# Gate and up strips of two FFNs: one matmul over 128 rows, or two row tiles of 64 rows side by side

## The chip, the cores and the metric

The kernel runs on one core of one Trainium2 chip. The metric is the device time in microseconds (us) of one execution, from the first to the last instruction; lower is better. The core has five engines that run their own instruction queues: TensorE (PE in the profile, with its weight loads listed apart as PEld), VectorE (DVE), ScalarE (ACT), GpSimd (POOL) and SyncE (SP, which here issues the DMAs). Matmuls read weights and moving data from SBUF and write sums to PSUM, of which this kernel uses eight banks: four tiles named acc and four named sm.

## The reference

One layer of a decoder step, in fp32, on 320 tokens (256 of a prompt, 64 of samples), model width 2048, FFN width 5632:

```python
x = x + 0.5 * swiglu_ffn(rmsnorm(x, n_f1), f1_g, f1_u, f1_d)     # (silu(h @ wg) * (h @ wu)) @ wd
m, s_new, buf_new = mixer(rmsnorm(x, n_mix), ...)                # HGRN2 heads + conv module
x = x + m
x = x + cross_attn(rmsnorm(x, n_xa), mk, mv, xa_q, xa_o)
x = x + 0.5 * swiglu_ffn(rmsnorm(x, n_f2), f2_g, f2_u, f2_d)
y = rmsnorm(x, final)
```

Only the products with the gate and up weights (2048 x 5632 each, in both FFNs) are touched by the change.

## The kernel before

Activations stand transposed: 16 tiles `xs[k]` of 128 features by T = 320 tokens. Weights stream from HBM in units of 128 x 1024 (tile `raw`, 512 KB, three buffers). ACT casts each unit to fp32r (`whi`, L116), DVE computes the rest that the cast lost (`wlo`, L117), and both go to TensorE; `whi` and `wlo` have four buffers each. Activations are split in the same way: `xgh`, `xgl` for the inputs of a projection, `hh`, `hl` for the FFN's inner values.

`mm3` (L176 to L178) multiplies one 128 x 128 block of weights with 320 tokens in three fp32r matmuls that add up in one PSUM bank: whi by xh, whi by xl, wlo by xh. `strip` makes one strip of 128 output features: 16 blocks, so 48 matmuls over two units.

`ffn` runs the FFN in six parts of 8, 8, 8, 8, 8 and 4 strips (`PARTS`). Within a part it makes a gate strip and an up strip for each of the eight; after the gate strip DVE multiplies the PSUM sum with `r`, the inverse root mean square (tile fa, L242), ACT takes Silu (L243), DVE multiplies by `r` again (L244); after the up strip DVE multiplies its PSUM sum with that (tile fb, L249) and `split` makes hh on ACT and hl on DVE. Then come the part's down products: 16 sums `ps` of 24 matmuls each (12 in the last part), which DVE adds to `xs[n]` (L259). One FFN thus has 88 strips, 4224 matmuls, and 2112 matmuls of down products.

The order on each engine is set by a scheduler at build time: instructions follow the program's order as far as their inputs are expected to be there; the units' fetches (DMA, L116, L117) have high priority and so stand early. Each engine then runs its queue strictly in that order. The rest of the program, about a quarter of the time between the FFNs, is the mixer and the cross attention; there are short fp32 matmuls among its strips (L512, L514, L584 and others), which run in two passes each. Some of them are already laid out on parts of the array: L584 takes 64 rows at a time, alternately the lower and the upper half of the partitions, into two PSUM tiles, and L556, L742 and L770 use 32 columns at a time.

Of the kernel before, what the change touches and what calls it, by code (L numbers as in the profile page):

```python
# [14 lines left out]
ALU = mybir.AluOpType  # L15
AX = mybir.AxisListType

P = 128
DM = 2048
KT = DM // P  # L20
# [4 lines left out]
T = NP + NS  # L25
# [37 lines left out]
def hymba(tc, A, O):  # L63
    nc = tc.nc
    count = [0]

    def tl(pool, shape, dt, tag, bufs):
        count[0] += 1
        return pool.tile(shape, dt, tag=tag, name=f"{tag}_{count[0]}", bufs=bufs)
# [9 lines left out]
    with (  # L79
# [8 lines left out]
        def acc():  # L88
            return tl(pp, [P, 512], F32, "acc", 4)

        def sm():
            return tl(pp, [P, 512], F32, "sm", 4)
# [6 lines left out]
        eps = cp.tile([P, 1], F32, name="eps")  # L99
# [15 lines left out]
        def split(hi, lo, src):  # L115
            nc.scalar.copy(hi, src)  # L116
            nc.vector.tensor_tensor(lo, src, hi.bitcast(F32), ALU.subtract)  # L117

        def pair(tag, w=T):
            return (tl(mp, [P, w], F32R, tag + "h", 16), tl(mp, [P, w], F32R, tag + "l", 17 if tag == "h" else 16))  # L120
# [5 lines left out]
        def fetch(early=False):  # L126
            with contextlib.nullcontext() if early else tc.high_priority():
                raw = tl(mp, [P, 1024], F32, "raw", 3)
                g, u = divmod(fetched[0], 2)
                nc.sync.dma_start(raw, A["w"][g, :, u * 1024 : (u + 1) * 1024])  # L130
                hi = tl(mp, [P, 1024], F32R, "whi", 4)
                lo = tl(mp, [P, 1024], F32R, "wlo", 4)
                split(hi, lo, raw)
                units.append((hi, lo))
            fetched[0] += 1

        def unit():
            while fetched[0] < 2 * G_TOT and fetched[0] < upos[0] + 4:
                fetch()
            u = units[upos[0]]  # L140
            units[upos[0]] = None
            upos[0] += 1
            return u
# [3 lines left out]
        def pump():  # L147
            for q in queues:
                q["due"] = q.get("due", 0) + q["rate"]
                while q["due"] >= 1:  # L150
                    q["due"] -= 1
                    while q["jobs"]:
                        try:
                            next(q["jobs"][0])
                            break
                        except StopIteration:
                            q["jobs"].pop(0)
# [9 lines left out]
        def tick(n):  # L167
            mms[0] += n
            if mms[0] >= pace[0]:
                mms[0] -= pace[0]  # L170
                pump()

        def mm3(out, w, kk, xh, xl, first, last):
            hi = w[0][:, kk * P : (kk + 1) * P]
            lo = w[1][:, kk * P : (kk + 1) * P]
            nc.tensor.matmul(out, hi, xh, start=first, stop=False)  # L176
            nc.tensor.matmul(out, hi, xl, start=False, stop=False)  # L177
            nc.tensor.matmul(out, lo, xh, start=False, stop=last)  # L178
            tick(1)

        def strip(xg, ps):
            for half in range(2):
                w = unit()
                for kk in range(8):
                    k = half * 8 + kk
                    mm3(ps, w, kk, *xg[k], k == 0, k == KT - 1)

        # r = (ps / n + eps) ** -0.5, the tables' value and one step of Newton's
        def root(r, ps, n):
            v = tl(mp, [P, r.shape[-1]], F32, "sq", 2)  # L190
            a = sm()[:, : r.shape[-1]]
# [40 lines left out]
        def ffn(pool, xg, root_of, done, setup=None):  # L232
            for pi, np_ in enumerate(PARTS):
                last_part = pi == len(PARTS) - 1
                hs = []
                for _ in range(np_):
                    pg = acc()
                    strip(xg, pg[:, :T])
                    if pi == 0 and not hs:
                        r = root_of()  # L240
                    t = tl(pool, [P, T], F32, "fa", 2)
                    nc.vector.tensor_tensor(t, pg[:, :T], r, ALU.mult)  # L242
                    nc.scalar.activation(t, t, AF.Silu)  # L243
                    nc.vector.tensor_tensor(t, t, r, ALU.mult)  # L244
                    pu = acc()
                    strip(xg, pu[:, :T])
                    hp = pair("h")
                    h = tl(pool, [P, T], F32, "fb", 2)
                    nc.vector.tensor_tensor(h, pu[:, :T], t, ALU.mult)  # L249
                    split(*hp, h)  # L250
                    hs.append(hp)
                w = None
                for n in range(KT):
                    if n * np_ % 8 == 0:
                        w = unit()
                    ps = acc()
                    for kk in range(np_):
                        mm3(ps[:, :T], w, n * np_ % 8 + kk, *hs[kk], kk == 0, kk == np_ - 1)
                    nc.vector.scalar_tensor_tensor(xs[n], ps[:, :T], 0.5, xs[n], ALU.mult, ALU.add)  # L259
                    if last_part:  # L260
                        done(n)
                if pi == 0 and setup is not None:
                    setup(pool)

        # first FFN
        nc.gpsimd.memset(ones, 1.0)
        nc.gpsimd.memset(eps, EPS)

# [6 lines left out]
        def setup(fp):  # L275
            nc.sync.dma_start(ident, A["ident"])
            nc.sync.dma_start(vmask, A["vmask"])
            nc.sync.dma_start(sel, A["sel"])
            for i0 in range(0, len(LEVELS), 3):
                i1 = min(i0 + 3, len(LEVELS))  # L280
                t = tl(fp, [P, 3, T], F32, "t4k", 2)
                nc.sync.dma_start(t[:, : i1 - i0], A["msk"][:, i0:i1, :])
                nc.vector.tensor_copy(msk[:, i0:i1, :], t[:, : i1 - i0])
            nc.gpsimd.memset(at[0], 0.0)
            nc.gpsimd.memset(at[1], 0.0)

            l0 = vec[:, V_LB : V_LB + NH]
            l1 = vec[:, V_LB + NH : V_LB + 2 * NH]
            lmax = cp.tile([P, NH], F32, name="lmax")
            le0 = cp.tile([P, NH], F32, name="le0")  # L290
            le1 = cp.tile([P, NH], F32, name="le1")
            nc.vector.tensor_tensor(lmax, l0, l1, ALU.max)
            nc.vector.tensor_tensor(le0, l0, lmax, ALU.subtract)
            nc.vector.tensor_tensor(le1, l1, lmax, ALU.subtract)
            nc.scalar.activation(le0, le0, AF.Exp)
            nc.scalar.activation(le1, le1, AF.Exp)
            nc.vector.tensor_tensor(le1, le0, le1, ALU.add)
            nc.vector.reciprocal(le1, le1)
            nc.vector.tensor_tensor(lb, le0, le1, ALU.mult)
            nc.vector.tensor_scalar(oml, lb, -1.0, 1.0, ALU.mult, ALU.add)  # L300
            nc.vector.tensor_scalar(noml, lb, 1.0, None, ALU.subtract)

            # the memory's root mean square
            mtot = tl(fp, [P, 1024], F32, "mtot", 1)
            for g in range(4):
                m = tl(fp, [P, 1024], F32, "t4k", 2)
                nc.sync.dma_start(m, A["mem"][:, g, :])
                if g == 0:
                    nc.scalar.activation(mtot, m, AF.Square)
                else:  # L310
                    nc.scalar.activation(m, m, AF.Square)
                    nc.gpsimd.tensor_tensor(mtot, mtot, m, ALU.add)
            nc.gpsimd.tensor_tensor(mtot[:, :512], mtot[:, :512], mtot[:, 512:], ALU.add)
            nc.gpsimd.tensor_tensor(mtot[:, :MEM], mtot[:, :MEM], mtot[:, MEM:512], ALU.add)
            ps = sm()
            nc.tensor.matmul(ps[:, :MEM], ones, mtot[:, :MEM], start=True, stop=True)
            root(rmem, ps[:, :MEM], DM)

        with phase("ffn1") as fp:
            nc.sync.dma_start(vec, A["vec"])  # L320
            xg = []
# [8 lines left out]
        with phase("mixer") as wk:  # L330
# [1 line left out]
            def tmp(tag, bufs=2, w=T):  # L332
                return tl(wk, [P, w], F32, tag, bufs)

            # a projection of the prompt's memory, tokens on the partitions
            def mem_proj(tag, between=None):
                pv = [acc() for _ in range(2)]
                for k in range(KT):
# [22 lines left out]
            r = roots[0]  # L361
# [4 lines left out]
            xg = []  # L366
            for k in range(KT):
                t = tmp("gt")
# [270 lines left out]
            for h in range(XH):  # L639
                ps = sm()  # L640
                for mt in range(2):
                    s = slice(mt * P, (mt + 1) * P)
# [6 lines left out]
            xg = []  # L649
            for part in range(2):  # L650
                if part:
                    drain()
                for n in range(KT):
                    ps = acc()
                    w = unit()
# [4 lines left out]
                        xg.append(scaled_split(n, "xattn"))  # L660
                        stat.add(xs[n])

        # cross attention
        with phase("xattn") as ap:
            scale = float(128.0**-0.5)
            roots = []
# [137 lines left out]
            xg = []  # L804
            for n in range(KT):
                if n % 2 == 0:
                    w = unit()
                ps = acc()
# [3 lines left out]
                xg.append(scaled_split(n, "ffn2"))  # L812
                stat.add(xs[n])

        # second FFN
        with phase("ffn2") as fp:
            prev, stat1 = stat, Stat(True)

# [8 lines left out]
            r = stat1.rstd()  # L827
# [150 lines left out]
```

## Time and profile before

| | |
|---|---|
| median of three runs | 2580.84 us (2579.68 to 2581.11) |
| span of the profiled execution | 2581.1 us |
| PE busy | 2538.0 us, 98%, 17280 matmuls |
| PEld busy | 2491.3 us, 97%, 17280 weight loads |
| DVE busy | 1473.7 us, 57% |
| ACT busy | 1076.9 us, 42% |
| POOL busy | 100.1 us, 4% |
| DMA | 397.37 MB, mean 154 GB/s |

The profiled execution's span of 2581.1 us is the same time as the slowest of the three runs, 2581.11 us, and 0.3 us above their median. In the profile's rows a matmul's duration reaches from its start to the modelled end of its last result, so the durations of neighbours overlap; what one costs in a stream is the distance from its start to the next one's start. A row of the timeline gives start, duration, engine, line, operation, names, shapes and how many instructions were merged into it. `64*128` beside a matmul are the rows and columns of the array that it uses.

### The profile page before, as it was taken

The numbers are of one execution on the slowest core, as the hardware profiler recorded it, in microseconds if no ns is written. First come the engines' busy times: TensorE is split into PE (matmuls) and PEld (weight loads), VectorE is DVE, ScalarE is ACT, GpSimd is POOL, SyncE is SP. The second block draws the span as 40 slices with busy tenths as digits, with TensorE's granted clock in tenths as the row PEclk, the third lists the DMA queues.
The fourth block names the chain that finished last, engine by engine and source line by source line (L and its number), as shares of the span: only waits on it lengthen the run. The fifth ranks groups of instructions, "written<-read, shape, count | busy, mean of one in ns | idle before, by whom it ended". The sixth has DMA issues, their size and how long they took to land.

```text
span 2581.1 us, 41685 instructions
## 1 busy us (share of the span) xinstructions
PE 2538.0 (98%) x17280; PEld 2491.3 (97%) x17280; DVE 1473.7 (57%) x2110; ACT 1076.9 (42%) x1487; POOL 100.1 (4%) x105
## 2 busy tenths in 40 slices
PE   7999999999999999999999999999999999999997
PEld 7999999999999989999998898999999999999997
DVE  6544444444444478788878775744444444444444
ACT  6333333333233354565655744532333333333334
POOL 4000000000000020000000020200000000000002
PEclk9999999999999999999999999999999999999999
DMA  7444444444444465444444554444444444444443
GB/s 234 156 151 150 148 150 152 148 150 152 148 149 153 148 195 160 146 156 141 150 144 146 198 176 150 147 152 148 150 152 148 150 152 148 150 153 148 150 152 107
DMA packets 111790, 397.37 MB, mean 154 GB/s; under 512 B 12656, under 2 KB 16368, under 8 KB 111600
## 3 DMA queue, kind: packets, MB, share of 16 engines
q1 hardware_dynamic: 111600, 394.70, 48.1%
q8 instruction: 136, 2.23, 0.3%
q14 instruction: 54, 0.44, 0.0%
HBM read 384.90 MB, written 9.76 MB: 153 GB/s over the span
## 4 chain that ended last, share of the span: by engine, by line
PE 92%; DVE 4%; ACT 2%; issue 1%; DMA 0%; POOL 0%; DVEq 0%; ACTq 0%; POOLq 0%
PE acc L176 29%; PE acc L177 29%; PE acc L178 29%; DVE wlo L117 1%; PE sm L512 1%; PE sm L605 1%; ACT whi L116 0%; DVE xgl L229 0%; DVE t L343 0%; PE sm L571 0%; ACT L194 0%; DVE hl L117 0%; ACT t L549 0%; DVE x L811 0%; PE sm L616 0%
## 5 line engine op out<-in xcount | busy, mean ns | idle before, releaser
L116 ACT CAST whi<-raw 128x1024 fp32r<-128x1024 f32 x688 | 721.7, 1049 | 1369.4 <-PE acc L177 983.7
L117 DVE TENSOR_TENSOR wlo<-raw,whi 128x1024 fp32r<-128x1024 f32 x688 | 849.6, 1235 | 557.2 <-ACT whi L116 556.7
L176 PE MATMUL acc<-xgh,whi 128*128 128x320 f32 x3648 | 1140.5, 313 | 11.5 <-ACT whi L116 9.4
L177 PE MATMUL acc<-xgl,whi 128*128 128x320 f32 x3648 | 1130.6, 310 | 3.5 <-DVE xgl L117 1.9
L178 PE MATMUL acc<-xgh,wlo 128*128 128x320 f32 x3648 | 1129.7, 310 | 1.8 <-DVE wlo L117 1.8
L176 PEld LDWEIGHTS acc<-xgh,whi 128*128 128x128 f32 x3648 | 686.8, 188 | 17.2 <-ACT whi L116 9.4
L177 PEld LDWEIGHTS acc<-xgl,whi 128*128 128x128 f32 x3648 | 687.2, 188 | 7.0 <-DVE xgl L229 3.2
L178 PEld LDWEIGHTS acc<-xgh,wlo 128*128 128x128 f32 x3648 | 686.7, 188 | 2.5 <-DVE wlo L117 2.5
L176 PE MATMUL acc<-hh,whi 128*128 128x320 f32 x1728 | 534.3, 310 | 2.4 <-DVE x L658 1.5
L178 PE MATMUL acc<-hh,wlo 128*128 128x320 f32 x1728 | 534.5, 309 | 0.0
L177 PE MATMUL acc<-hl,whi 128*128 128x320 f32 x1728 | 533.9, 309 | 0.0
L176 PEld LDWEIGHTS acc<-hh,whi 128*128 128x128 f32 x1728 | 324.1, 188 | 4.6 <-issue 3.0
L177 PEld LDWEIGHTS acc<-hl,whi 128*128 128x128 f32 x1728 | 324.3, 188 | 0.3 <-issue 0.2
L178 PEld LDWEIGHTS acc<-hh,wlo 128*128 128x128 f32 x1728 | 324.3, 188 | 0.2
L259 DVE SCALAR_TENSOR_TENSOR x<-acc,x 128x320 f32<-128x320 f32 x192 | 94.0, 491 | 223.0 <-PE acc L178 222.9
L212 POOL TENSOR_TENSOR ssq<-ssq,sq 128x320 f32<-128x320 f32 x74 | 83.8, 1133 | 1925.2 <-ACT sq L210 1021.0
L411 DVE SCALAR_TENSOR_TENSOR hl<-u,vec,hl 128x256 f32<-128x256 f32 x240 | 115.4, 481 | 2.3
L249 DVE TENSOR_TENSOR fb<-acc,fa 128x320 f32<-128x320 f32 x88 | 43.3, 492 | 111.0 <-PE acc L178 110.9
L242 DVE TENSOR_TENSOR fa<-acc,r 128x320 f32<-128x320 f32 x88 | 43.2, 492 | 109.1 <-PE acc L178 109.0
L229 DVE SCALAR_TENSOR_TENSOR xgl<-x,vec,xgh 128x320 fp32r<-128x320 f32 x48 | 47.3, 1016 | 0.9 <-ACT xgh L228 0.9
L117 DVE TENSOR_TENSOR hl<-fb,hh 128x320 fp32r<-128x320 f32 x88 | 43.2, 491 | 0.0
L244 DVE TENSOR_TENSOR fa<-fa,r 128x320 f32<-128x320 f32 x88 | 42.6, 485 | 0.6 <-ACT fa L243 0.6
(198 smaller groups left out, 1029.7 us busy)
## 6 DMA issues: line engine op xcount, KB each, us to landing
raw<-in_w SPq DMA_DIRECT2D x688, 512.0 KB, 3.8
t<-in_mem SPq DMA_DIRECT2D x8, 512.0 KB, 5.9
t<-in_s SPq DMA_DIRECT2D x8, 512.0 KB, 4.9
out_ss<-t SPq DMA_DIRECT2D x8, 512.0 KB, 3.6
kv<-in_ck SPq DMA_DIRECT2D x8, 512.0 KB, 6.3
kv<-in_cv SPq DMA_DIRECT2D x8, 512.0 KB, 6.2
t4k<-in_mem SPq DMA_DIRECT2D x4, 512.0 KB, 5.0
x<-in_x SPq DMA_DIRECT2D x3, 640.0 KB, 6.9
```

The source lines that it names most:

```text
L116: nc.scalar.copy(hi, src)
L117: nc.vector.tensor_tensor(lo, src, hi.bitcast(F32), ALU.subtract)
L176: nc.tensor.matmul(out, hi, xh, start=first, stop=False)
L177: nc.tensor.matmul(out, hi, xl, start=False, stop=False)
L178: nc.tensor.matmul(out, lo, xh, start=False, stop=last)
L212: nc.gpsimd.tensor_tensor(self.total, self.total, s, ALU.add)
L229: nc.vector.scalar_tensor_tensor(l, xs[k], norm(name, k), h.bitcast(F32), ALU.mult, ALU.subtract)
L242: nc.vector.tensor_tensor(t, pg[:, :T], r, ALU.mult)
L244: nc.vector.tensor_tensor(t, t, r, ALU.mult)
L249: nc.vector.tensor_tensor(h, pu[:, :T], t, ALU.mult)
L259: nc.vector.scalar_tensor_tensor(xs[n], ps[:, :T], 0.5, xs[n], ALU.mult, ALU.add)
L411: nc.vector.scalar_tensor_tensor(dw[:, :NP], u[:, j : j + NP], cw, dw[:, :NP], ALU.mult, ALU.add)
```

## The change

The gate and up strips of both FFNs go through a new function, `strip_rows`, in place of `strip`. Each 128-row block is cut into rows 0 to 63 and rows 64 to 127, and each of the three products becomes two matmuls of 64 rows, one for each half, with the same 128 output columns and the same 320 tokens. The lower halves add up in one acc tile (`pa`), the upper halves in another (`pb`). A strip is then 96 matmuls. After a strip, ACT copies `pa` to SBUF and DVE adds `pb` to it; the multiplication that read PSUM before now reads SBUF. The down products, the mixer and the cross attention keep `strip` and `mm3`.

```diff
+        def strip_rows(xg, pa, pb):
+            rows = slice(0, 64), slice(64, P)
+            for half in range(2):
+                w = unit()
+                for kk in range(8):
+                    k = half * 8 + kk
+                    cs = slice(kk * P, (kk + 1) * P)
+                    for i, (wi, xi) in enumerate(((0, 0), (0, 1), (1, 0))):
+                        for r, ps in zip(rows, (pa, pb)):
+                            nc.tensor.matmul(
+                                ps,
+                                w[wi][r, cs],
+                                xg[k][xi][r, :],
+                                start=k == 0 and i == 0,
+                                stop=k == KT - 1 and i == 2,
+                            )
+                    tick(1)
...
-                    pg = acc()
-                    strip(xg, pg[:, :T])
+                    pg = acc(), acc()
+                    strip_rows(xg, pg[0][:, :T], pg[1][:, :T])
...
-                    nc.vector.tensor_tensor(t, pg[:, :T], r, ALU.mult)
+                    nc.scalar.copy(t, pg[0][:, :T])
+                    nc.vector.tensor_tensor(t, pg[1][:, :T], t, ALU.add)
+                    nc.vector.tensor_tensor(t, t, r, ALU.mult)
...
-                    pu = acc()
-                    strip(xg, pu[:, :T])
+                    pu = acc(), acc()
+                    strip_rows(xg, pu[0][:, :T], pu[1][:, :T])
...
-                    nc.vector.tensor_tensor(h, pu[:, :T], t, ALU.mult)
+                    nc.scalar.copy(h, pu[0][:, :T])
+                    nc.vector.tensor_tensor(h, pu[1][:, :T], h, ALU.add)
+                    nc.vector.tensor_tensor(h, h, t, ALU.mult)
```

The order of instructions that results, at three places. Names carry the number of the buffer or of the tile's use; an acc tile that appears twice with the same number is the same sum.

First, TensorE within the last gate strip of the first FFN's first part, before: three matmuls for each block, all into one acc tile.

```order
L176 MATMUL acc_188_1158<-xgh_25_141,whi_180_1094 128x320
L177 MATMUL acc_188_1158<-xgl_26_142,whi_180_1094 128x320
L178 MATMUL acc_188_1158<-xgh_25_141,wlo_181_1095 128x320
L176 MATMUL acc_188_1158<-xgh_27_145,whi_180_1094 128x320
L177 MATMUL acc_188_1158<-xgl_28_146,whi_180_1094 128x320
```

TensorE at the start of the last up strip of the same part, after: six matmuls for each block, lower and upper half in turn (acc 211 and 212).

```order
L198 MATMUL acc_211_1988<-xgh_4_96,whi_197_1812 128x320
L198 MATMUL acc_212_1989<-xgh_4_96,whi_197_1812 128x320
L198 MATMUL acc_211_1988<-xgl_5_97,whi_197_1812 128x320
L198 MATMUL acc_212_1989<-xgl_5_97,whi_197_1812 128x320
L198 MATMUL acc_211_1988<-xgh_4_96,wlo_198_1813 128x320
L198 MATMUL acc_212_1989<-xgh_4_96,wlo_198_1813 128x320
L198 MATMUL acc_211_1988<-xgh_6_101,whi_197_1812 128x320
```

The halves stay in turn nearly everywhere: among the 16,896 matmuls of L198 there are five places, all in the first two strips, where two matmuls of the same half follow each other. On TensorE's queue the program changes 27 times between matmuls of 64 rows and of 128 rows.

Second, TensorE where the down products of that first part begin, before: the last strip's inner values (hh 203, hl 204) are used by the 22nd to the 24th matmul of the first sum, acc 209.

```order
L178 MATMUL acc_209_1296<-hh_185_1152,wlo_194_1192 128x320
L176 MATMUL acc_209_1296<-hh_203_1284,whi_193_1191 128x320
L177 MATMUL acc_209_1296<-hl_204_1285,whi_193_1191 128x320
L178 MATMUL acc_209_1296<-hh_203_1284,wlo_194_1192 128x320
L176 MATMUL acc_213_1328<-hh_77_360,whi_198_1226 128x320
```

The same place on TensorE after: the last strip's values are hh 219 and hl 220, the first two sums acc 225 and 229.

```order
L178 MATMUL acc_225_2112<-hh_199_1864,wlo_209_1931 128x320
L176 MATMUL acc_229_2144<-hh_79_460,whi_214_1992 128x320
L177 MATMUL acc_229_2144<-hl_80_461,whi_214_1992 128x320
L178 MATMUL acc_229_2144<-hh_79_460,wlo_215_1993 128x320
L176 MATMUL acc_229_2144<-hh_99_694,whi_214_1992 128x320
L176 MATMUL acc_225_2112<-hh_219_2098,whi_208_1930 128x320
L177 MATMUL acc_229_2144<-hl_100_695,whi_214_1992 128x320
L178 MATMUL acc_229_2144<-hh_99_694,wlo_215_1993 128x320
L177 MATMUL acc_225_2112<-hl_220_2099,whi_208_1930 128x320
L178 MATMUL acc_225_2112<-hh_219_2098,wlo_209_1931 128x320
```

The scheduler has put six matmuls of the second sum ahead of the last ones of the first: hh 219 is now used by the 26th matmul and hl 220 by the 29th. The other parts of eight strips have the same pattern.

Third, DVE around the last up strip of that part, before: the multiplication out of PSUM (L249), one weight unit's wlo, hl, and then the first down sum's addition to x.

```order
L117 TENSOR_TENSOR wlo_202_1257<-raw_200_1254,whi_201_1256 128x1024
L249 TENSOR_TENSOR fb_205_1286<-acc_196_1223,fa_195_1219 128x320
L117 TENSOR_TENSOR wlo_208_1293<-raw_206_1290,whi_207_1292 128x1024
L117 TENSOR_TENSOR hl_204_1285<-fb_205_1286,hh_203_1284 128x320
L259 SCALAR_TENSOR_TENSOR x0_65<-acc_209_1296,x0_65 128x320
```

DVE at the same place after: both weight units' wlo stand ahead of the addition out of PSUM (L271), the multiplication (L272) and hl.

```order
L117 TENSOR_TENSOR wlo_218_2047<-raw_216_2044,whi_217_2046 128x1024
L117 TENSOR_TENSOR wlo_224_2109<-raw_222_2106,whi_223_2108 128x1024
L271 TENSOR_TENSOR fb_221_2100<-acc_212_1989,fb_221_2100 128x320
L272 TENSOR_TENSOR fb_221_2100<-fb_221_2100,fa_210_1982 128x320
L117 TENSOR_TENSOR hl_220_2099<-fb_221_2100,hh_219_2098 128x320
L282 SCALAR_TENSOR_TENSOR x0_65<-acc_225_2112,x0_65 128x320
```

ACT at that place after the change: the new copy stands behind both casts of weight units, with hh right behind it.

```order
L116 CAST whi_217_2046<-raw_216_2044 128x1024
L116 CAST whi_223_2108<-raw_222_2106 128x1024
L270 COPY fb_221_2100<-acc_211_1988 128x320
L116 CAST hh_219_2098<-fb_221_2100 128x320
L116 CAST whi_227_2140<-raw_226_2138 128x1024
```

So the way from a strip's last matmul to hl has gained a copy on ACT and an addition on DVE, and on DVE it has moved behind one more wlo.

## Prediction

> **What bounds the kernel now.** I read the page's first part and its chain, then the busy time by stage, then TensorE's timeline.
>
> ```profile
> PE 2538.0 (98%) x17280; PEld 2491.3 (97%) x17280; DVE 1473.7 (57%) x2110; ACT 1076.9 (42%) x1487; POOL 100.1 (4%) x105
> PE 92%; DVE 4%; ACT 2%; issue 1%; DMA 0%; POOL 0%; DVEq 0%; ACTq 0%; POOLq 0%
> 60.00:932.00 872.00, 872.00 (x5945) 871.76 (x5944) 424.07 (x504) 298.46 (x345) 9.99 (x10) 1.00 0.48 151
> 1640.00:2560.00 920.00, 919.64 (x6267) 919.02 (x6267) 444.43 (x532) 322.31 (x381) 12.09 (x12) 1.00 0.47 148
> ```
>
> The last two rows are stretches of the two FFNs: length, then busy time and count of PE, PEld, DVE, ACT and POOL, then the granted clock. TensorE hardly stops there: 872.00 us by 5945 matmuls is 146.7 ns each, and 919.64 by 6267 is 146.7 again. The FFNs cost what their matmuls cost; DVE is idle for half of the time and ACT for two thirds. The timeline shows one such slot, and two others to compare it with:
>
> ```profile
> 300.03 0.31 PE L177 MATMUL acc<-xgl,whi 128*128 128x320 f32 x1
> 300.03 0.19 PEld L178 LDWEIGHTS acc<-xgh,wlo 128*128 128x128 f32 x1
> 300.17 0.31 PE L178 MATMUL acc<-xgh,wlo 128*128 128x320 f32 x1
> 953.14 0.39 PE L351 MATMUL acc<-whi,hh 128*128 128x512 f32 x1
> ...
> 957.00 0.39 PE L353 MATMUL acc<-whi,hl 128*128 128x512 f32 x1
> ...
> 11.35 0.47 PE L177 MATMUL acc<-xgl,whi 128*128 128x320 f32 x1
> 11.62 0.47 PE L178 MATMUL acc<-xgh,wlo 128*128 128x320 f32 x1
> ```
>
> The weights of the next matmul start to load as the present one starts, so loads already run beside matmuls. With 320 columns the starts stand 0.147 us apart; with 512 columns 3.86 us for 17 slots, 0.227 each: 0.080 us for 192 more columns is 0.417 ns a column. So 320 columns are 133.3 ns, and 13.3 ns of each slot are fixed. At the kernel's start the slot is 0.267 us, 320 columns at twice 0.417 ns and nothing over: when the array is slower, the fixed part hides. It is a matter of feeding the array, and not array cycles.
>
> **The main term: a pair of half matmuls.** 2 x 4224 = 8448 slots become 8448 pairs. The trace has no fp32r row tiles, but fp32 ones (L584, two passes for each of four matmuls, halves in turn), beside an fp32 group of whole rows (L512), and fp32 column tiles (L742) beside whole matmuls of the same 256 columns (L711):
>
> ```profile
> 1053.21 0.31 PE L178 MATMUL acc<-xgh,wlo 128*128 128x320 f32 x1
> 1053.45 0.38 PE L584 MATMUL sm<-vt,ket 64*128 64x128 f32 x2
> ...
> 1053.45 0.49 PE L584 MATMUL sm<-vt,ket 64*128 64x128 f32 x4
> ...
> 1053.45 0.71 PE L584 MATMUL sm<-vt,ket 64*128 64x128 f32 x8
> 1054.10 0.41 PE L176 MATMUL acc<-xgh,whi 128*128 128x320 f32 x1
> 1054.35 0.30 PE L177 MATMUL acc<-xgl,whi 128*128 128x320 f32 x1
> ...
> L584 PE MATMUL sm<-vt,ket x8: 272/272/373, 1053.5 to 1053.9; 64*128 64x128 f32 x8
> 1031.95 0.31 PE L178 MATMUL acc<-xgh,wlo 128*128 128x320 f32 x1
> 1032.10 0.60 PE L512 MATMUL sm<-qk 128*128 128x128 f32 x4
> 1032.46 0.39 PE L176 MATMUL acc<-xgh,whi 128*128 128x320 f32 x1
> 1032.69 0.31 PE L177 MATMUL acc<-xgl,whi 128*128 128x320 f32 x1
> ...
> 1572.34 1.03 PE L711 MATMUL sm<-kT,q 128*128 128x256 f32 x4
> 1573.30 1.93 PE L742 MATMUL sm<-kv,qm 128*32 128x256 f32 x32
> ```
>
> The first pair of L584 has ended after 0.38 us, the second after 0.49, the fourth after 0.71: one pair each 0.11 us. A whole L512 takes (0.60 - 0.27) / 3 = 0.11 us as well (0.27 is one duration). So two halves cost what one whole costs. L742 shows it with longer streams: 32 passes start within 1.93 - 0.38 = 1.55 us, eight groups of four each 0.2 us, where one whole pass of L711 takes (1.03 - 0.38) / 3 = 0.217 us (0.38 as in the 512-column rows). Four at once cost one.
>
> I take 146.7 ns for a pair of fp32r halves: no gain, no loss, because a strip streams its 320 tokens 48 times as before, whether through one tile or two. The bounds: from below the fixed 13.3 ns is gone (133.3 ns; 8448 x 13.3 = -112 us), from above the halves run one after the other (293 ns; 8448 x 146.7 = +1239 us). The rows lie on the value that I take; their weakness is that fp32 streams a column in 0.83 ns (0.217 us by 256), half the rate of fp32r.
>
> **Changing the mode.** From the strip matmul before L584 to the second one behind it are 1054.35 - 1053.21 = 1.14 us; two slots of 0.147 and four pairs of 0.11 are 0.73. So 0.40 us went for one change to row tiles and one back. The same sum for L512 is 1032.69 - 1031.95 = 0.74 against 0.73: fp32 between fp32r costs nothing, the tiling costs. 27 changes by 0.20 us are **+5.4 us**. The Trainium skill, TensorEngine Tiling (Array Packing), Key Properties, says that changing the tiling mode drains TensorE; the rows above agree and give the price. The same page (The Problem) sees the array underused where the contracted dimension is 64 or less; here it is 128, so by that page there is nothing to win either.
>
> **The five places** of one half twice running cost at most a slot each: **+0.5 us** of at most 0.7.
>
> **From the last strip to the down products.** The copy is priced by a Silu of the same size, the addition by L249; the rest is the transition at 302 us:
>
> ```profile
> L243 ACT ACTIVATE fa<-fa 128x320 f32<-128x320 f32 x88 | 40.8, 465 | 0.0
> L249 DVE TENSOR_TENSOR fb<-acc,fa 128x320 f32<-128x320 f32 x88 | 43.3, 492 | 111.0 <-PE acc L178 110.9
> 301.93 0.31 PE L178 MATMUL acc<-xgh,wlo 128*128 128x320 f32 x1
> 302.08 0.31 PE L176 MATMUL acc<-hh,whi 128*128 128x320 f32 x1
> 302.18 1.05 ACT L116 CAST whi<-raw 128x1024 fp32r<-128x1024 f32 x1 [2.47 <-PE acc L177]
> 302.28 0.49 DVE L249 TENSOR_TENSOR fb<-acc,fa 128x320 f32<-128x320 f32 x1 [1.31 <-PE acc L178]
> 303.13 0.45 ACT L116 CAST hh<-fb 128x320 fp32r<-128x320 f32 x1
> 303.26 1.23 DVE L117 TENSOR_TENSOR wlo<-raw,whi 128x1024 fp32r<-128x1024 f32 x1 [0.49 <-ACT whi L116]
> 304.40 0.48 DVE L117 TENSOR_TENSOR hl<-fb,hh 128x320 fp32r<-128x320 f32 x1
> ```
>
> Counted from the last strip matmul (301.93): hl ends at 2.95, and its first user, the 23rd down matmul, starts at 0.15 + 22 x 0.147 = 3.38. No stall. After the change the copy takes the place of hh behind the whi that frees at the strip's end: 1.20 to 1.66. DVE does wlo from 1.33; the addition starts at 2.47 (where hl did), the multiplication at 2.95, hh at 3.5, hl ends at 4.44. TensorE starts the down products at 0.34 (0.24 as from 1053.21 to 1053.45, and 0.10 for the first weights, as the 0.38 of the first pair is 0.10 longer than a pass); hh is used by the 26th matmul, 0.34 + 25 x 0.147 = 4.0, hl by the 29th, 4.45. It just fits. With twelve transitions, two of them in the short last parts, I put a sixth of a us on each, **+2 us**; 0 if it fits, 6 if each is half a us late.
>
> **Hidden work.** 176 copies x 0.465 = 82 us on ACT and 176 additions x 0.49 = 86 us on DVE lie in their idle time. Behind a waiting copy on ACT stand casts of units that are needed a strip (7.0 us) later. The pair of PSUM tiles is free 2.95 us after its strip, and needed 7.0 us after. If that cover were gone, each strip would wait for its copy and addition, 0.465 + 0.492 us, 168 us in all. 16,896 more PE instructions (a load and a matmul for each added half) make 4 in 146.7 ns, 37 ns each; TensorE has taken 130 in 1.96 us:
>
> ```profile
> 1603.45:1605.41 1.96, 1.96 (x65) 1.76 (x65) 0.06 (x1) 0.00 (x0) 0.00 (x0) 1.00 0.00 0
> ```
>
> **Sum.** 2581.1 + 5.4 + 0.5 + 2 = 2589.0; the median is 0.3 below the profiled run, so 2588.7, about 2589 us (+0.3%). What a measurement of this kernel can tell from no change is 0.2%, 5.2 us.
>
> **Rivals.**
> *The feed is shared.* If the fixed 13.3 ns must be paid for each half, one after the other, a pair takes 160 ns: 2589 + 8448 x 13.3 ns = 2701 us; if a part of it is paid, something between. For it: the fixed part is feeding, and in the fp32 rows the slow columns hide it as they do at 11 us. Against: L742's groups show no such addition. 0.20.
> *The halves run one after the other.* At full rate two streams may not fit where two at half rate do: 2589 + 1239 = 3828 us. That the change doesn't do what it says would look like this. Against: L584 and L742. 0.10.
> *The fixed part hides* (the other side): if it comes of a weight load that takes the feed of its own rows, a load for the other half lets this half stream on. Wholly gone it is 2589 - 112 = 2477 us; from 0.9 ns a pair (7.9 us by 8448) it outweighs the rest. For it: the slot at 11 us. Against: each half must still load once in its own slot. 0.10. The Trainium skill, TensorE: Matmul & The Clock Gate, The mechanism, says that weight loads overlap running matmuls only when the row group differs, which speaks for this rival. The rows at 300.03, load and matmul of the same rows at once, don't agree, so it gets no more than that.
>
> **How the numbers follow.** The forecast, pairs at 146.7 ns, has 0.60 and by itself 2582 to 2600. The range adds the shared feed at full price, 2582 to 2705, and leaves out the last two rivals, 0.20 together. Faster is the third rival, 0.10. Within 0.2% the forecast falls below 2586, where the transitions fit and changes of mode are cheaper than 0.2: 0.14. Slower is the rest, 0.76.
>
> **What would show it.** In the changed profile: L198 twice within 0.02 us, then 0.147 us on; PE's busy time in the FFN's strips as before; 0.1 us more at each end of a row-tile stretch, and again for the first weights; waits of L176 for hh or hl below 0.5 us at the down products. A pair distance other than 0.147 makes the prediction wrong at once: 1 ns is 8.4 us.

## The result, and the profile after

The changed kernel takes 2598.8 us (median, 2598.25 to 2599.63) against 2580.26 us (2579.01 to 2581.11) of the kernel before: 18.5 us more, a ratio of 1.0073 (95% interval 1.0061 to 1.0086). The profiled span is 2597.4 us, 16.3 above the one before. The direction was forecast, but the change costs more than twice the 8 us that the prediction summed. One execution of one of the runs below (the kernel before with the changed order) took 4396 us at a granted clock of 0.70 and is left out of that run's figures.

Most of it happened as forecast. Lines of the page, then of TensorE's timeline, then a stretch of row-tile strips in the first FFN after the change and one of the same length before (length, then busy time and count of PE, PEld, DVE, ACT, POOL, then the granted clock):

```profile
span 2597.4 us, 58846 instructions
PE 2549.0 (98%) x25728; PEld 2494.5 (96%) x25728; DVE 1559.5 (60%) x2286; ACT 1132.9 (44%) x1663; POOL 97.0 (4%) x105
PEclk8999999999999999999999999999999999999999
```

```profile
299.92 0.31 PE L198 MATMUL acc<-xgh,whi 64*128 64x320 f32 x2
300.06 0.31 PE L198 MATMUL acc<-xgl,whi 64*128 64x320 f32 x2
300.21 0.31 PE L198 MATMUL acc<-xgh,wlo 64*128 64x320 f32 x2
```

```profile
202.00:313.00 111.00, 111.00 (x1518) 111.00 (x1516) 60.74 (x79) 48.06 (x68) 0.00 (x0) 1.00 0.46 150
```

```profile
190.00:301.00 111.00, 111.00 (x759) 111.00 (x758) 53.57 (x64) 43.67 (x54) 0.00 (x0) 1.00 0.47 150
```

Two halves go out together (x2) and the next two 0.147 us later. In 111 us there are 1518 half matmuls, 759 pairs, where there were 759 whole ones. TensorE has 8448 matmuls more and does the same work in the same time. DVE's 86 us more are the additions. The clock's first slice is 8, where it was 9 in all of them before; that slice is the subject of what follows below.

The ends of a row-tile stretch, first to the down products, then back:

```profile
313.85 0.31 PE L198 MATMUL acc<-xgh,wlo 64*128 64x320 f32 x2
314.09 0.42 PE L176 MATMUL acc<-hh,whi 128*128 128x320 f32 x1
314.34 0.31 PE L177 MATMUL acc<-hl,whi 128*128 128x320 f32 x1
...
370.57 0.31 PE L178 MATMUL acc<-hh,wlo 128*128 128x320 f32 x1
370.81 0.42 PE L198 MATMUL acc<-xgh,whi 64*128 64x320 f32 x2
371.06 0.31 PE L198 MATMUL acc<-xgl,whi 64*128 64x320 f32 x2
```

Either way two starts take 0.49 us where two slots take 0.293: 0.195 us a change (unrounded starts), 0.20 in the sum.

The chain behind the last strip (which ends with the matmul at 313.85), on ACT, DVE and TensorE:

```profile
315.05 0.42 ACT L270 COPY fb<-acc 128x320 f32<-128x320 f32 x1
316.32 0.48 DVE L271 TENSOR_TENSOR fb<-acc,fb 128x320 f32<-128x320 f32 x1
316.84 0.49 DVE L272 TENSOR_TENSOR fb<-fb,fa 128x320 f32<-128x320 f32 x1
317.36 0.46 ACT L116 CAST hh<-fb 128x320 fp32r<-128x320 f32 x1 [1.90 <-DVE fb L272]
317.86 0.49 DVE L117 TENSOR_TENSOR hl<-fb,hh 128x320 fp32r<-128x320 f32 x1 [0.53 <-ACT hh L116]
...
318.42 0.40 PE L177 MATMUL acc<-hl,whi 128*128 128x320 f32 x1
318.65 0.30 PE L178 MATMUL acc<-hh,wlo 128*128 128x320 f32 x1
```

From 313.85 on, the copy starts after 1.20 us, the addition after 2.47, hl ends after 4.50. The prediction had 1.20, 2.47 and 4.44. hl's first user starts after 4.57 where the order alone would let it at 4.45; hh is late by as little. Together that is 0.2 us for each of twelve transitions.

**What the prediction did not look at is the start.** From the first strip matmul to the first matmul of the down products, in one window each, before and then after:

```profile
9.39:132.70 123.31, 117.96 (x771) 115.51 (x771) 77.08 (x90) 63.85 (x92) 30.80 (x24) 1.00 0.59 192
```

```profile
9.13:144.11 134.98, 124.33 (x1538) 121.04 (x1539) 84.42 (x105) 68.08 (x107) 28.93 (x24) 0.95 0.54 177
```

The same eight gate and eight up strips take 134.98 us in place of 123.31, 11.7 more (the first down product comes 11.4 later, as the first strip begins 0.26 earlier). TensorE idles for 10.65 us in place of 5.35, and is busy for 6.4 us longer with the same number of slots. The clock column tells why: 0.95 in place of 1.00. Three stretches are at half:

```profile
21.10:28.00 6.90, 6.61 (x45) 6.21 (x47) 5.12 (x11) 4.88 (x11) 4.62 (x6) 0.51 0.58 210
34.80:38.20 3.40, 3.40 (x30) 3.40 (x28) 1.64 (x4) 3.37 (x7) 0.00 (x0) 0.50 0.66 171
58.70:62.10 3.40, 3.40 (x30) 3.40 (x28) 2.73 (x3) 2.40 (x4) 0.00 (x0) 0.50 0.42 145
```

The counts also hold matmuls that only reach into a stretch. At the edges of the last one stand these rows:

```profile
58.60 0.64 PE L198 MATMUL acc<-xgh,wlo 64*128 64x320 f32 x2
...
62.19 0.44 PE L198 MATMUL acc<-xgl,whi 64*128 64x320 f32 x2
```

Fourteen pairs start in these 3.59 us (0.267 us apart inside the stretch), where fourteen slots of 0.147 take 2.05: the stretch costs 1.5 us. Each stretch follows a wait. TensorE's waits in the first 80 us, before and then after (who waited, for what; us in all, times, longest):

```profile
PE acc L176 <- ACT xgh L228: 1.4, 1, 1.4
PE sm L219 <- POOL ssq L212: 0.9, 1, 0.9
```

```profile
PE acc L198 <- ACT xgh L247: 3.0, 1, 3.0
PE acc L198 <- DVE fa L262: 2.8, 1, 2.8
PE sm L238 <- POOL ssq L231: 2.0, 1, 2.0
```

Two waits are longer, and the one for fa (L262, the new addition) is new: it is a wait for PSUM. The other waits there (for the first weights and their wlo) are alike in both. So these waits cost twice: their own length, and half pace after it.

The rest of the 16.3 us: 27 changes of mode 5.3, twelve transitions 2.4, and the mixer's stretch, from the first FFN's last down product to the next L176 with hh, is 2.2 shorter (446.13 in place of 448.35 us). With 11.4 from the start that is 16.9. The mixer's 2.2 us go with the clock: before, 13.7 us of that stretch are at half clock (two spells of 6.8), now 6.8 (two of 3.4). Over all the profiles of this document it takes 446.0 to 446.2 us with 6.8 us at half clock and 442.9 to 445.0 with 3.4, and there are kernels without row tiles in both groups. Without that term the sum is 19.1, beside 18.5 between the medians.

### The profile page after: what moved, and what is told of

Same layout as the page of the kernel before. It is cut to its first block, busy times and chain, and to the rows that moved or that the text cites. A ratio compares the mean times of both kernels' runs of the same rounds, so it can differ in the third digit from the quotient of the medians.

```text
span 2597.4 us, 58846 instructions
## 1 busy us (share of the span) xinstructions
PE 2549.0 (98%) x25728; PEld 2494.5 (96%) x25728; DVE 1559.5 (60%) x2286; ACT 1132.9 (44%) x1663; POOL 97.0 (4%) x105
## 4 chain that ended last, share of the span: by engine, by line
PE 92%; DVE 4%; ACT 2%; issue 1%; DMA 1%; POOL 0%; DVEq 0%; SPq 0%; ACTq 0%; POOLq 0%
PE acc L198 47%; PE acc L176 14%; PE acc L177 13%; PE acc L178 13%; DVE wlo L117 1%; PE sm L535 1%; PE sm L628 1%; ACT whi L116 1%; POOL ssq L231 0%; DMA raw<-in_w 0%; DVE xgl L248 0%; PE sm L594 0%; DVE t L366 0%; ACT L213 0%; DVE hl L117 0%
## 5 line engine op out<-in xcount | busy, mean ns | idle before, releaser
L198 PE MATMUL acc<-xgh,whi 64*128 64x320 f32 x5632 | 912.0, 308 | 15.3 <-ACT whi L116 9.1
L198 PE MATMUL acc<-xgh,wlo 64*128 64x320 f32 x5632 | 909.6, 307 | 2.0 <-DVE wlo L117 2.0
L198 PE MATMUL acc<-xgl,whi 64*128 64x320 f32 x5632 | 910.1, 307 | 1.3 <-DVE xgl L248 1.2
L198 PEld LDWEIGHTS acc<-xgh,whi 64*128 64x128 f32 x5632 | 566.7, 185 | 19.4 <-ACT whi L116 9.4
L198 PEld LDWEIGHTS acc<-xgl,whi 64*128 64x128 f32 x5632 | 566.6, 185 | 2.5 <-DVE xgl L248 2.4
L198 PEld LDWEIGHTS acc<-xgh,wlo 64*128 64x128 f32 x5632 | 566.3, 185 | 2.6 <-DVE wlo L117 2.6
L176 PE MATMUL acc<-hh,whi 128*128 128x320 f32 x1728 | 534.8, 311 | 2.6 <-DVE x L681 1.6
L176 PEld LDWEIGHTS acc<-hh,whi 128*128 128x128 f32 x1728 | 323.9, 188 | 8.4 <-issue 5.4
L176 PE MATMUL acc<-xgh,whi 128*128 128x320 f32 x832 | 268.4, 323 | 0.4 <-ACT xgh L116 0.4
L177 PE MATMUL acc<-xgl,whi 128*128 128x320 f32 x832 | 258.1, 310 | 1.9 <-DVE xgl L117 1.9
L178 PE MATMUL acc<-xgh,wlo 128*128 128x320 f32 x832 | 257.8, 310 | 0.0
L176 PEld LDWEIGHTS acc<-xgh,whi 128*128 128x128 f32 x832 | 157.1, 189 | 5.3 <-issue 2.8
L177 PEld LDWEIGHTS acc<-xgl,whi 128*128 128x128 f32 x832 | 157.2, 189 | 3.5 <-DVE xgl L117 2.4
```

Source lines behind the costliest of these rows:

```text
L198: nc.tensor.matmul(ps, w[wi][r, cs], xg[k][xi][r, :], start=k == 0 and i == 0, stop=k == KT - 1 and i == 2,)
```

## The experiments

The question is what makes the start slow: that a strip now takes two of the four acc tiles (theory A at first), the longer chain behind it, or the row tiles; later also the order of the first strips (theory E), and three separate waits (theory G). Each run was timed against the kernel before on its own chip (medians 2580.09, 2579.86 and 2581.01 us in three groups of runs). "Start" is the stretch of 123.31 and 134.98 us above.

**Row tiles in the second FFN alone.** `ffn` uses `strip` and the old lines where `setup` is given, which it is in the first FFN.

```diff
-                    pg = acc(), acc()
-                    strip_rows(xg, pg[0][:, :T], pg[1][:, :T])
+                    pg = (acc(), acc()) if setup is None else (acc(),)
+                    if setup is None:
+                        strip_rows(xg, pg[0][:, :T], pg[1][:, :T])
+                    else:
+                        strip(xg, pg[0][:, :T])
```

> Row tiles in the second FFN only; the first FFN is as before. Theory A (most of the loss is made in the first 144 us, where strips wait for their inputs and only two strips, not four, have PSUM tiles): 14 changes of mode x 0.20 = 2.8 us and 6 transitions to down products x 0.2 = 1.2 us, so +4.0 us, about 2584.3 us, ratio 1.0016. Rival B (the loss is spread evenly over the strips of both FFNs): half of +18.5, about 2589.5 us, ratio 1.0036.

Measured: 2584.95 us, ratio 1.0019 (1.0010 to 1.0028). With the first FFN as before the start is 123.30 us again, and what is left is what changes of mode and transitions of one FFN cost. Most of the loss is in the first FFN, and half of the strips in row tiles cost 4.9 us.

**Two PSUM tiles without row tiles.** Whole rows, even blocks into one acc tile and odd ones into the other, with the copy and the addition of the change.

```diff
+                    mm3(pb if k % 2 else pa, w, kk, *xg[k], k < 2, k >= KT - 2)
```

> No row tiles: whole rows, blocks of even number summed in one PSUM tile and of odd number in the other, with the copy and the addition of the changed kernel. Theory A: the start loses as in the changed kernel, +11.4 us, and 12 transitions x 0.2 = 2.4 us, no change of mode: +13.8 us, about 2594.1 us, ratio 1.0054. Rival C (row tiles themselves, by their doubled loads and matmuls or by the clock, cost the start): only the transitions, about 2582.7 us, ratio 1.0009.

Measured: 2583.57 us, ratio 1.0015 (1.0006 to 1.0024); start 126.51. Theory A fell: pairs of PSUM tiles without row tiles cost 3.2 us of the 11.7. None of TensorE's waits there is for PSUM; one more wait for xgh (1.0 us) and a half-clock stretch (31.9 to 35.3 us) are what came in. The row tiles or the order that comes with them must be in the rest.

**The longer chain without the second PSUM tile.** Whole rows into one acc tile; ACT copies it, DVE takes the maximum of it and its copy, then the multiplication.

```diff
-                    nc.vector.tensor_tensor(t, pg[:, :T], r, ALU.mult)
+                    nc.scalar.copy(t, pg[:, :T])
+                    nc.vector.tensor_tensor(t, pg[:, :T], t, ALU.max)
+                    nc.vector.tensor_tensor(t, t, r, ALU.mult)
```

> No row tiles and one PSUM tile for each strip, but the longer way out of PSUM: ACT copies the sum, DVE takes the larger of the sum and its copy (the same value), then multiplies from SBUF. Theory A: four strips in flight again, so the start loses nothing; 12 transitions x 0.2 = 2.4 us, about 2582.7 us, ratio 1.0009. Rival D (the added copy and addition in the queues of ACT and DVE hold up the start): +11.4 + 2.4, about 2594.1 us, ratio 1.0054.

Measured: 2584.44 us, ratio 1.0018 (1.0009 to 1.0027); start 123.30. The chain costs the start nothing. A whole part of eight strips' down products takes 56.57 us in place of 56.32, so it costs 0.25 us a transition: that term needs no row tiles. Nor does it come with every such chain. In the run with two PSUM tiles the same part takes 56.32 us as before; ACT's copy there starts ahead of the cast of a weight unit (at 305.48 and 305.81 us), here and in the changed kernel behind it.

**The first four strips whole.** As the changed kernel, with `strip` and one acc tile for the first two gate and two up strips.

```diff
+                    rowt = setup is None or pi > 0 or len(hs) >= 2
```

> Row tiles in both FFNs, but the first four strips of the first FFN as whole rows in one PSUM tile each. Theory A: the start is as before, the rest of the price stays: 26 changes of mode x 0.20 = 5.2 us and 12 transitions x 0.2 = 2.4 us, +7.6 us, about 2587.9 us, ratio 1.0029; down products of the first part begin near 132.9 us instead of 144.1. Rival B: four of 176 strips matter little, about 2598 us, ratio 1.007.

Measured: 2590.12 us, ratio 1.0038 (1.0025 to 1.0050); start 126.64. Eight of the 11.7 us come back. What is left is a wait of 2.1 us for fa (L267) at 63 us, in the first strips with pairs, and a half-clock stretch at 22.8 to 26.2 us:

```profile
22.80:26.20 3.40, 3.40 (x13) 3.40 (x14) 3.37 (x7) 2.23 (x5) 1.78 (x2) 0.50 0.62 243
65.40:72.00 6.60, 6.60 (x90) 6.60 (x92) 5.05 (x7) 3.50 (x6) 1.94 (x6) 1.00 0.49 152
```

The clock stays at 1.00 behind the wait of 2.1 us. The half pace stands behind a wait of 1.4 us for xgh, which the kernel before has too, without half pace after it. So whether a wait of this size is followed by half pace differs from one profile to the next, and a start read from one profile can be off by the 1.5 us of such a stretch.

**The order of the first strips, two ways.** In the changed queue strip 2 has four slots ahead of the place where strip 1's second half holds the queue; before it had 15, which fill the time in which inputs arrive. First, the program of the changed kernel writes the first two strips half by half in turn.

```diff
+                        for half in range(2):
+                            rows_half(xg, pg[0][:, :T], pg[1][:, :T], w4[half], half)
+                            rows_half(xg, pu[0][:, :T], pu[1][:, :T], w4[2 + half], half)
```

> As the changed kernel, but the program itself writes the first two strips half by half in turn: first half of strip 1, first half of strip 2, second half of strip 1, second half of strip 2. In the changed kernel the build-time scheduler let strip 2 have 4 slots before strip 1 waited for its second half, in the kernel before 15. Theory E (the loss at the start is this order): most of the 11.4 us come back, about 8, so 2590.5 us, ratio 1.0040. Rival F (row tiles themselves make the start slow, by their number of instructions or by the clock): 2598.8 us, ratio 1.0072.

Measured: 2601.84 us, ratio 1.0084 (1.0070 to 1.0098); start 137.28. A miss: the wait for xgh became 4.2 us, and three waits for PSUM came in, one for strip 2's pair (fb, 1.4) and two for strip 3's (fa, 2.2 each). Strip 2 ends at 37.3 us, but ACT copies its sum (L280) only at 46.93. In ACT's queue that copy stands behind the square of the memory's first block, for whose DMA ACT waits 5.66 us, and behind the root's own work. So this edit lengthened the waits for xgh and for PSUM, and says nothing for or against theory E.

Second, the kernel before with its first two strips forced into the changed kernel's order.

```diff
+            for s, n in [(0, 24), (1, 4), (0, 1), (1, 1), (0, 11), (1, 10), (0, 1), (1, 1), (0, 11)]:
+                run(s, n)
+            r = root_of()
+            run(1, 32)
```

> The kernel before, no row tiles, with the first two strips forced into the order that the changed kernel has (24 slots of strip 1, 4 of strip 2, 1, 1, 11, 10, 1, 1, 11, then strip 2), and the third strip behind them. Theory E: the start loses 8 to 11 us, 2588 to 2591 us, ratio 1.003 to 1.0043, with idle time at 15 to 22 us and a stretch at half pace. Rival F: 2580 us, ratio 1.000.

Measured: 2584.6 us, ratio 1.0021 (1.0012 to 1.0031); start 127.75, +4.5, about half of what theory E expected. No row tile and no second PSUM tile is in it. The order here includes that strip 3 waits for strip 2's end, where the kernel before begins it during strip 1. The window of 15 to 40 us, of this run and of the kernel before:

```profile
15.00:40.00 25.00, 17.77 (x90) 15.43 (x89) 16.34 (x22) 17.62 (x32) 16.06 (x13) 0.86 0.64 209
```

```profile
15.00:40.00 25.00, 20.01 (x122) 17.97 (x121) 19.62 (x23) 18.86 (x32) 16.94 (x13) 1.00 0.69 227
```

90 matmuls in place of 122, with the clock at 0.86: the order alone brings the idle spell and the half pace behind it. The rest had to come from elsewhere.

**The other two waits.** The theory now was that the start holds three separate losses: the order, the root matmul (L238) that waits for POOL in the middle of strip 2, and the wait for fa at 55 us. For the last, POOL, DVE and ACT of the changed kernel, where strip 3's pair should come free (the strip ends at 47.8 us):

```profile
49.13 5.04 POOL L335 TENSOR_TENSOR mtot<-mtot,t4k 128x1024 f32<-128x1024 f32 x2 [2.88 <-ACT t4k L334]
52.22 5.24 DVE L117 TENSOR_TENSOR wlo<-raw,whi 128x1024 fp32r<-128x1024 f32 x2 [0.32 <-ACT whi L116]
53.04 0.41 ACT L261 COPY fa<-acc 128x320 f32<-128x320 f32 x1
57.38 0.48 DVE L262 TENSOR_TENSOR fa<-acc,fa 128x320 f32<-128x320 f32 x1
```

POOL adds up the squares of the memory (two additions, 5.04 us); DVE's two wlo take 2.62 us each, where they take 1.23 on the average; the addition L262 stands behind them, and the fifth strip, which needs this pair, waits. First, these sums are left out: the squares and their sums are replaced by a constant.

```diff
-            for g in range(4):
...
+            nc.vector.memset(mtot[:, :MEM], 16.0)
```

> As the changed kernel, without the squares and sums of the prompt's memory that ACT, POOL and DMA do at 45 to 60 us (a constant stands in their place, so the memory's norm is not computed). Theory G: the third strip is then taken out of PSUM in time and the fifth does not wait: 4 us less, about 2594.6 us, ratio 1.0055, no half pace at 58 us. If two strips' PSUM tiles are too few by themselves: the wait at 55 us stays, 2598.8 us, ratio 1.0072.

Measured: 2593.85 us, ratio 1.0053 (1.0041 to 1.0066); start 130.42, 4.6 us less. The window of 40 to 65 us, changed kernel and this one:

```profile
40.00:65.00 25.00, 22.24 (x284) 21.98 (x282) 17.95 (x18) 12.70 (x18) 11.52 (x9) 0.93 0.57 183
```

```profile
40.00:65.00 25.00, 25.00 (x346) 25.00 (x344) 14.65 (x20) 11.33 (x16) 0.00 (x0) 1.00 0.44 149
```

346 half matmuls in place of 284, no wait, full clock. POOL's, ACT's and the DMAs' share all went with the sums, so the run doesn't tell which of them made wlo slow. The changed kernel's profile points at POOL: all six wlo above 1.3 us (1.4 to 3.0) run beside a tensor operation on POOL, and none of the 649 without one beside it takes more than 1.23; but 33 others beside one are not slow.

Second, the root matmul alone is moved behind strip 2.

```diff
+                    if early:
+                        pu = acc(), acc()
+                        strip_rows(xg, pu[0][:, :T], pu[1][:, :T])
+                        hold.append(last_mm[0])
+                    if pi == 0 and not hs:
+                        r = root_of()
```

> As the changed kernel, but the matmul of the first root mean square stands behind the second strip on TensorE's queue, where the changed kernel has it in the middle of that strip. Theory G (the start's 11.4 us are three things: the order of the first two strips, 4.5; that matmul's wait for POOL with the second strip behind it, and the half pace that follows, some 3; the wait of the fifth strip for PSUM, and the half pace that follows, some 4): 3 us less, about 2595.8 us, ratio 1.0060, no idle time and no half pace at 30 to 38 us. If the wait for POOL only hides another: 2598.8 us, ratio 1.0072.

Measured: 2602.72 us, ratio 1.0086 (1.0072 to 1.0100); start 137.86. A miss in sign. The wait for POOL is gone, and TensorE waits twice for PSUM (36 to 75 us): for strip 2's pair (fb, new) and for strip 3's (fa, as in the changed kernel, 2.8 there):

```profile
PE acc L201 <- ACT fb L281: 3.5, 1, 3.5
PE acc L201 <- DVE fa L266: 2.3, 1, 2.3
```

ACT shows why strip 2's pair, whose strip ended at 36.1 us, comes free late:

```profile
41.46 1.06 ACT L343 ACTIVATE mtot<-t4k 128x1024 f32<-128x1024 f32 x1 [7.05 <-DMA t4k<-in_mem]
47.40 0.41 ACT L281 COPY fb<-acc 128x320 f32<-128x320 f32 x1
```

Moving the root also moved ACT's part of it (L214, at 44.77 us) behind the first square of the memory, and that square waits 7.05 us for its DMA. The copy L281 stands behind both.

Third, both edits together.

> The edits of the late root and of the missing memory sums together in the changed kernel. Theory G: only the order of the first two strips is left of the start, 4.5 us, with mode changes and transitions 7.6: about 2592 us, ratio 1.0046. If the two waits share a cause: not better than the better of the two alone.

Measured: 2590.19 us, ratio 1.0038 (1.0025 to 1.0051); start 126.80. With the memory's sums away, ACT copies strip 2's sum at 41.62 us in place of 47.40, and moving the root does bring 3.6 us (130.42 to 126.80). The two are not independent: an early strip 3 is of use only if the pairs come free. What is left, 3.5 us, is near what the order costs by itself (4.5).

**The whole first part as before.** Row tiles from the second part of the first FFN on.

```diff
+                    rowt = setup is None or pi > 0
```

> Row tiles everywhere but in the first FFN's first part (16 strips of 176), which is as before. Theory G: the whole start is as before, what is left is 25 changes of mode x 0.20 = 5.0 us and 11 transitions x 0.2 = 2.2 us, +7.2 us, about 2587.2 us, ratio 1.0028, and down products of the first part near 132.9 us. If the steady strips have a price of their own: 90% of 18.7 us, about 2597 us.

Measured: 2587.82 us, ratio 1.0026 (1.0016 to 1.0037); start 123.28. The row

```profile
132.32 0.31 PE L176 MATMUL acc<-hh,whi 128*128 128x320 f32 x1
```

stands where it stood before (132.70). By the ratios, 0.0073 - 0.0026 is 12 us of the 18.5: the start is the larger part of the loss.

**The price of a change of mode.** Each strip's first unit as row tiles, its second as whole rows into the lower half's tile: 359 changes in place of 27.

```diff
+            w = unit()
+            for kk in range(8):
+                mm3(pa, w, kk, *xg[8 + kk], False, kk == 7)
```

> Each strip's first unit in row tiles, its second unit in whole rows: 359 changes of mode in place of 27. At 0.195 us each, as the changed kernel's trace has it, 332 more are +65 us: about 2664 us. If a change only costs where the queue is short of work anyway: about 2599 us.

Measured in one execution: 2661.35 us, 62.6 more than the changed kernel by 332 more changes: 0.19 us each. Inside a stretch of 16 strips:

```profile
380.17:499.01 118.84, 118.84 (x1153) 112.86 (x1153) 60.49 (x78) 45.22 (x62) 0.00 (x0) 1.00 0.42 143
```

Two thirds of 1153 are 769 slots, 112.8 us at 0.1467; the 6.1 us over are 32 changes at 0.19.

**Three lower halves, then three upper.** The two inner loops are swapped, so that neighbours in the queue use the same half.

```diff
-                    for i, (wi, xi) in enumerate(((0, 0), (0, 1), (1, 0))):
-                        for r, ps in zip(rows, (pa, pb)):
+                    for r, ps in zip(rows, (pa, pb)):
+                        for i, (wi, xi) in enumerate(((0, 0), (0, 1), (1, 0))):
```

> The same half matmuls, but for each block three of the lower half, then three of the upper half. If matmuls start in the order of the queue, only every third can run beside its neighbour, a block takes 4 slots and not 3: 2816 blocks x 146.7 ns = +413 us, about 3012 us. If the array takes the halves from the queue as they fit: 2599 us. If halves ran side by side for another reason than their order, anything else.

Measured in one execution: 2595.86 us.

```profile
399.84 0.32 PE L198 MATMUL acc<-xgh,whi 64*128 64x320 f32 x2
399.99 0.32 PE L198 MATMUL acc<-xgl,whi 64*128 64x320 f32 x2
400.13 0.32 PE L198 MATMUL acc<-xgh,wlo 64*128 64x320 f32 x2
```

Still two halves at a time, a pair each 0.147 us. In this kernel's queue three matmuls into one acc tile are followed by three into the other, as the program writes them, so an upper half starts ahead of two lower ones that stand before it. The halves need not be neighbours in the queue, and that each engine runs its queue strictly in order, as said of the kernel before, does not hold for TensorE here.

## Why the prediction was right, and where it was wrong

- **The main term** holds: a pair costs 146.7 ns, as one whole matmul. *The feed is shared* (160), *The halves run one after the other* (293) and *The fixed part hides* (below 146) are all refuted by the spacing of the pairs. The Trainium skill's rule beside that last rival (TensorE: Matmul & The Clock Gate, The mechanism) is that weight loads overlap running matmuls only when the row group differs. These rows don't agree: halves of different rows in turn are no faster than whole rows.
- **Changing the mode**: 27 changes at 0.195 us, 5.3 for the 5.4 of the sum. The fp32 rows of L584 gave the right price for fp32r.
- **From the last strip to the down products**: 2.4 us for 2; the chain ran within 0.1 us of its forecast.
- **The five places**: the failed step, together with *Hidden work*. These places are all in the first two strips; they were priced as a slot each, 0.5 us, and not read as a sign that the queue of these strips had been rearranged. And *Hidden work* took its cover (the pair free after 2.95 us, needed after 7.0) from the middle of the FFN, where it holds, for the whole kernel. At the start pairs come free late, inputs arrive late, and strips are interleaved to fill the time. The sum had no term for that stretch, and it cost 11.4 us, more than all its terms together.
- What the start's 11.7 us consist of, by the runs: the order of the first two strips 3.5 to 4.5 (forced upon the kernel before: 4.5; left when the other two are gone: 3.5), the root matmul's wait and the half pace after it 3.6, the wait for a PSUM pair beside the memory's sums 4.6. The first alone is shown without row tiles. The other two depend on each other, as the root moved alone showed. Each figure is the difference of two profiles, with the uncertainty of a half-clock stretch said above, so the split is rough; that the start as a whole is the larger part, the medians show.
- **The range** of 2582 to 2705 held the time, and the forecast's own range, 2582 to 2600, held it at its very edge. That is luck: the time lies there because of a term that the prediction did not have. *Slower* was right, and for the reasons given, but these reasons are 7.7 us of the 18.5.

Open: why the queue of the first strips came out so. The second PSUM tile does not bring it by itself, as the run with whole rows and two tiles has 17 matmuls of strip 2 ahead of strip 1's second half. A cause that fits is that the scheduler's build-time estimate counts each half as a matmul of its own; no run varied that. Open too: why wlo takes 2.6 us while POOL adds, why only some waits of 1 to 3 us are followed by half pace, and what the fixed 13.3 ns in each slot are.

## What to carry to other kernels

Two row tiles of 64 give nothing where the contracted dimension fills all 128 rows: a pair costs what one whole matmul costs, and each change of mode costs 0.2 us, so keep the modes in long stretches or not at all. Price an edit not only in the steady middle: a tile more for each sum halves the number of sums in flight, and at the start, where inputs still arrive, TensorE came to wait for these tiles, which it did not do in the middle of the FFN. Where a build step sets the order, compare the first few hundred rows of each queue as well as the steady ones, the queues that free the tiles (ACT, DVE) among them; a few odd rows there are a sign to be priced by the waits around them, not by the slots.

## What the hardware did that was not expected

The two halves run beside each other whatever their order in the queue: three lower then three upper matmuls still went out in pairs each 146.7 ns (2595.86 us, where strict order was expected to give 3012). The Trainium skill, TensorE: Matmul & The Clock Gate, The mechanism, has matmuls start in strict program order with no reordering; for matmuls on different rows these rows don't agree, and the measurement decides.

Waits of 2.0 us (34 us) and 2.8 us (55 us) on TensorE were each followed by 3.4 us at half clock, which costs 1.5 us more. The Trainium skill, TensorE: Matmul & The Clock Gate, What's actually happening, puts the clock's window at about 3.4 us; the length of the stretches, 3.4 and 6.9 us, agrees, but here waits shorter than a window were enough. The wait's length does not decide it alone: in the run with the first four strips whole, a wait of 2.1 us was followed by none.
